# First projection of a two-block network from a feature-major copy of x, with the weight loads at the start of the queue

## The chip, the cores and the metric

One core of one Trainium2 chip runs the kernel. The metric is the device time of one execution in microseconds (us); shorter is better. TensorE is called PE, VectorE DVE, ScalarE ACT, GpSimd POOL, and SyncE, which issues nearly all DMAs here, SP.

## The reference, cut to what matters

256 tokens of 1024 features go through two blocks: an even layer (two attentions of 16 heads), an odd layer (retention) and a second block (state space, window attention, feed-forward). Only the head of the even layer matters here:

```python
def rms_norm(x, g):                       # per token
    y = xf * lax.rsqrt(jnp.mean(xf * xf, axis=-1, keepdims=True) + EPS)
    return y * g
z = rms_norm(x, g_norm) @ w_in            # [256, 1024] @ [1024, 8208]
qa, ka, va, ga, fa, qb, kb, vb, gb = jnp.split(z, cuts, axis=-1)
log_f = jax.nn.log_sigmoid(fa + b_f)      # forget gates, one a head
c = jnp.cumsum(log_f, axis=1)             # added to the logits of attention a, with the causal mask
y = concat([ya * silu(ga), yb * silu(gb)]); x = x + y @ w_out
```

The factor rsqrt(mean(x^2)) belongs to a token, so it can be put in after the product with the weights; the gain g belongs to a feature.

## The kernel before, in words

Every product with weights is done in three: the operands are split into a high part (float32r) and the rest, and high x high, low x high and high x low are summed in PSUM. A weight tile is [128, 1024] float32 (512 KB). `Weights` (lines 48 to 109) streams 233 such tiles in order of use: `load` (L63) issues the DMA on SP into one of five `wraw` buffers, `_prepare` makes the high part `wh` on ACT (L73, `nc.scalar.copy`) and the low part `wl` by a subtraction on DVE (L78; of some tiles on POOL) into a ring of six, and `next` hands a tile out and prepares two ahead. SP's queue holds eight DMAs in flight: a ninth waits for the landing of the first.

The even layer begins with x token-major: `load_x` (L131) brings each tile of 128 tokens in two halves, `norm_transposed` takes the squares (L202 on ACT, L199 on DVE), the factor on POOL (L191), multiplies by factor and gain (L215, the gain spread over the partitions by a product with ones, L598), transposes on PE (L235) and splits into `xTh`, `xTl` [128 features, 8, 256 tokens] (L242, L243). `first_xs` multiplies them by the four tiles of the first half of v (L289 for the high parts of the weights, L296 for their low parts; 48 products of 512 columns), with the second token tile's transposes in between. `forget_gates` follows: a product of 16 rows (24 products, L250 to L252), then a chain over DVE, ACT, DVE (scan, L637), POOL (L639), a DMA to `c_dram` (L640), DMAs back to all partitions (`fox_masks`, L645), and POOL (L648, L649). What it makes, `m`, is added to the scores by the first DVE operation of each head (L346, L348).

Then come, for each quarter i of a half, q, k and gate (`proj_ws`, 48 products of 256 columns each, two weight tiles), and the attention of four heads: scores of a pair (L338), minimum on DVE, exponentials on ACT, normalisation on DVE (L684 to L686), transposes on PE (L362), product with v (L372). Two PSUM banks (`bat`) hold the scores of a pair, so the next pair's scores wait for the DVE operation that reads the last ones (L348). q is scaled on ACT (L664), k copied on DVE (L667), the gate is a tanh on ACT (L670) and one operation on DVE (L671). The framework simulates the program and sets each engine's order of instructions from that; PE executes strictly in its order.

Of the kernel before, what the change touches and what calls it, by code (L numbers as in the profile page):

```python
# [19 lines left out]
P = 128  # L20
# [14 lines left out]
# of this many weight tiles of a part of the network, one has its lower part made on GpSimd (0: none)  # L35
SH = (0, 0, 2, 8)
KE = ("pp", "py")
XH = 2
# [7 lines left out]
class Weights:  # L46
    """Streams weight tiles [128, n] in order of use and splits each into two float32r parts."""

    def __init__(self, tc, raw, par, ahead):
        self.tc, self.nc, self.raw, self.par, self.ahead = tc, tc.nc, raw, par, ahead  # L50
        self.after, self.loaded, self.loads, self.lows = [], [], 0, []
        self.jobs, self.shares, self.done, self.used = [], [], [], 0

    def plan(self, aps, share=0):
        """share: one tile in so many has its lower part computed on GpSimd."""
        self.jobs += aps
        self.shares += [share] * len(aps)

    def load(self):
        ap = self.jobs[self.loads]  # L60
        self.loads += 1
        r = self.raw.tile([P, 1024], F32, tag="raw", name="wraw")
        self.nc.sync.dma_start(r[:, :ap.shape[1]], ap)  # L63
        self.loaded.append(r)

    def _prepare(self):
# [6 lines left out]
        i = nc.scalar.copy(h[:, :n], r[:, :n])  # L73
# [6 lines left out]

    def hold(self, first, second):
# [18 lines left out]
def model_kernel(ctx: ExitStack, tc: tile.TileContext, a: dict, out: bass.AP):  # L100
# [23 lines left out]
    g_row = nrm.tile([P, D], F32, tag="gain", name="g_row")  # L124
    nc.sync.dma_start(g_row[:1, :], a["even_norm"])
    x = [res.tile([P, D], F32, name=f"x{t}") for t in range(2)]

    def load_x(t):
        for h in range(XH):
            sl = slice(h * D // XH, (h + 1) * D // XH)  # L130
            nc.sync.dma_start(x[t][:, sl], a["x"][t * P:(t + 1) * P, sl])  # L131

    load_x(0)
# [36 lines left out]

    w.load()
    load_x(1)

# [20 lines left out]
    def mean_square(src, n, name, eng=None):  # L194
        """Sum of squares over the free dimension of src, divided by n."""
# [9 lines left out]
    def norm_transposed(t, g, th, tl, name, kinds=("pt", "pt"), eng=None, after=None):  # L205
        """The rows of x[t] normalised, times g, its halves, transposed into th, tl."""
        with tc.high_priority():
            xt = x[t]
            parts = [mean_square(xt[:, h * 512:(h + 1) * 512], D, name, eng if h else None) for h in range(2)]
            r = rstd_from(parts, EPS, name)  # L210
            xn = []
            for h in range(2):
                sl = slice(h * 512, (h + 1) * 512)
                xn.append(nrm.tile([P, 512], F32, tag="xn", bufs=3, name="xn"))
                V.scalar_tensor_tensor(xn[h], xt[:, sl], r, g[h], op0=ALU.mult, op1=ALU.mult)  # L215
            return transposed(xn, 8, th, tl, 0, t, kinds, after)

    def gained_transposed(t, g, kinds):
        """The rows of x[t] times g, its halves, transposed into xTh, xTl."""
# [9 lines left out]
    def transposed(src, n, th, tl, k0, t, kinds=("pt", "pt"), after=None):  # L229
        """src, a list of [128 tokens, 512], into th, tl [:, k0.., tokens of tile t] as two float32r parts."""  # L230
        m = min(4, n)
        for b, sb, kind in zip(range(0, n, 4), src, kinds):
            pt = bank(kind)
            for j in range(m):
                i = T.transpose(pt[:, j * P:(j + 1) * P], sb[:, j * P:(j + 1) * P], ident)  # L235
                if after is not None:
                    tc.add_manual_dep(i.ins, after.ins.name, NOSYNC, reason="order")
                    after = None
# [9 lines left out]

    def mm3(ps, lh, ll, rh, rl, first, last):
        T.matmul(ps, lh, rh, start=first, stop=False)  # L250
        T.matmul(ps, lh, rl, start=False, stop=False)  # L251
        T.matmul(ps, ll, rh, start=False, stop=last)  # L252

    def proj_ws(kind="pp"):
        """The next stationary weights times xT: PSUM [128 features, 2, 256 tokens]."""
# [24 lines left out]
    def first_xs(mid):  # L280
        """The first projection: the products of the weights' lower parts last, x's second token tile by mid."""
        tiles = [w.next() for _ in range(4)]
        ps = [bank("pp"), bank("pp")]
        for t in range(2):
            st = slice(t * P, (t + 1) * P)
            for g in range(0, 8, 2):
                for xp in (xTh, xTl):
                    for k in range(g, g + 2):
                        m = T.matmul(ps[t], xp[:, k, st], tiles[k // 2][0][:, 512 * (k % 2):512 * (k % 2) + 512],  # L289
                                     start=xp is xTh and k == 0, stop=False)  # L290
                        if t == 0 and xp is xTh and k == 1:
                            mid(m)
        for t in range(2):
            st = slice(t * P, (t + 1) * P)
            for k in range(8):
                T.matmul(ps[t], xTh[:, k, st], tiles[k // 2][1][:, 512 * (k % 2):512 * (k % 2) + 512],  # L296
                         start=False, stop=k == 7)
# [79 lines left out]
    # Chunks of four steps; two groups (a pair) share the 128 partitions, four pairs are a quarter.  # L377
# [6 lines left out]
    def reduce_angle(r, k, ang):  # L384
        """r: ang minus the nearest multiple of 2 pi; k: scratch."""
# [850 lines left out]
```

## Time and profile before

| | |
|---|---|
| time of three runs | 812.02, 811.92, 810.00 us; median 811.92 |
| span of the profiled execution (first to last instruction) | 810.7 us; its own time is not listed apart, and the median lies 1.2 us above the span |
| PE, share of the span | 96% |
| DVE, ACT, POOL | 69%, 50%, 29% |
| DMA | 146.46 MB, mean 181 GB/s |
| chain of work that ended last | PE 82%, DVE 5%, POOL 4%, issue 3%, ACT 3%, DMA 3% |

The span is cut into 40 slices of 20.3 us; PE's line reads 7, 9, 8 and from then on nearly always 9 or more. A matmul's listed duration includes a modelled end that overlaps with the next one, so how long a series takes is read from the starts. Times in the rows are counted from the span's start.

### The profile page before, as it was taken

How to read it: one execution, taken by the hardware profiler on the slowest of the kernel's cores; microseconds unless marked ns; L12 is line 12 of the kernel's file. 1: busy time of each engine (PE TensorE's matmuls, PEld its weight loads, DVE VectorE, ACT ScalarE, POOL GpSimd, SP SyncE). 2: the span in 40 equal slices, each digit the busy share in tenths (PEclk: the TensorE clock that was granted, in tenths of full speed). 3: DMA queues.
4: the chain of work that ended last, by engine and by line, in shares of the span. 5: the costliest groups of instructions: out<-in, count | busy, mean ns of one | idle time of the engine just before them, and what ended most of it. 6: DMA issues, size and time to landing. Idle time of an engine off the chain costs nothing.

```text
span 810.7 us, 13533 instructions
## 1 busy us (share of the span) xinstructions
PE 780.7 (96%) x5114; PEld 682.1 (84%) x5114; DVE 560.7 (69%) x1013; ACT 408.3 (50%) x680; POOL 237.2 (29%) x274
## 2 busy tenths in 40 slices
PE   7989999999999999999999999989798999999996
PEld 5978997998997789898989887876577999999886
DVE  6987668678778468585766757698849856565433
ACT  5766565457455355344444355736645544443331
POOL 4662111013604212120202006853653322221110
PEclk9999999999999999999999999999999999999999
DMA  7687544644744757453636494852243765555431
GB/s 284 222 270 234 172 165 131 208 150 154 238 161 133 234 186 254 154 188 124 208 119 194 151 334 152 301 195 85 81 127 110 235 200 177 189 183 181 156 130 53
DMA packets 47427, 146.46 MB, mean 181 GB/s; under 512 B 5361, under 2 KB 11777, under 8 KB 47362
## 3 DMA queue, kind: packets, MB, share of 16 engines
q1 hardware_dynamic: 47362, 145.60, 54.5%
q8 instruction: 40, 0.66, 0.3%
q14 instruction: 25, 0.20, 0.1%
HBM read 137.70 MB, written 7.88 MB: 180 GB/s over the span
## 4 chain that ended last, share of the span: by engine, by line
PE 82%; DVE 5%; POOL 4%; issue 3%; ACT 3%; DMA 3%; SPq 0%; POOLq 0%; DVEq 0%; ACTq 0%
PE bpp L274 12%; PE bpp L275 12%; PE bpp L278 12%; PE bpp L251 9%; PE bpp L250 9%; PE bpp L252 9%; PE bat L252 3%; PE bat L251 3%; PE bat L250 3%; PE bpy L372 2%; PE bat L338 2%; PE bpt L362 1%; PE bpp L289 1%; DVE wl L78 1%; POOL wl L78 1%
## 5 line engine op out<-in xcount | busy, mean ns | idle before, releaser
L78 DVE TENSOR_TENSOR wl<-wraw,wh 128x1024 fp32r<-128x1024 f32 x211 | 276.5, 1321 | 114.9 <-ACT wh L73 114.9
L73 ACT CAST wh<-wraw 128x1024 fp32r<-128x1024 f32 (+1 forms) x233 | 238.6, 1045 | 190.0 <-PE bpp L251 54.1
L251 PE MATMUL bpp<-xTl,wh 128*128 128x256 f32 (+1 forms) x680 | 193.3, 284 | 0.0
L250 PE MATMUL bpp<-xTh,wh 128*128 128x256 f32 (+1 forms) x680 | 193.1, 284 | 0.0
L252 PE MATMUL bpp<-xTh,wl 128*128 128x256 f32 (+1 forms) x680 | 192.9, 284 | 0.0
L251 PEld LDWEIGHTS bpp<-xTl,wh 128*128 128x128 f32 (+1 forms) x680 | 127.3, 187 | 2.6 <-issue 1.9
L250 PEld LDWEIGHTS bpp<-xTh,wh 128*128 128x128 f32 (+1 forms) x680 | 127.3, 187 | 1.8 <-issue 1.3
L252 PEld LDWEIGHTS bpp<-xTh,wl 128*128 128x128 f32 (+1 forms) x680 | 127.3, 187 | 1.0 <-issue 0.8
L274 PE MATMUL bpp<-wh,xTh 128*128 128x512 f32 (+1 forms) x288 | 110.9, 391 | 0.8 <-ACT xTh L242 0.8
L275 PE MATMUL bpp<-wl,xTh 128*128 128x512 f32 (+1 forms) x288 | 109.6, 385 | 0.0
L78 POOL TENSOR_TENSOR wl<-wraw,wh 128x1024 fp32r<-128x1024 f32 x22 | 57.7, 2624 | 62.9 <-ACT wh L73 62.9
L278 PE MATMUL bpp<-wh,xTl 128*128 128x512 f32 (+1 forms) x288 | 74.2, 382 | 0.0
L274 PEld LDWEIGHTS bpp<-wh,xTh 128*128 128x128 f32 x288 | 54.5, 190 | 13.3 <-ACT xTh L242 1.7
L275 PEld LDWEIGHTS bpp<-wl,xTh 128*128 128x128 f32 x288 | 54.5, 189 | 11.1 <-DVE wl L78 0.6
L278 PEld LDWEIGHTS bpp<-wh,xTl 128*128 128x128 f32 x288 | 52.2, 188 | 11.1
L274 PE MATMUL bpp<-wh,yh 128*128 128x512 f32 x128 | 50.5, 400 | 0.0
L275 PE MATMUL bpp<-wl,yh 128*128 128x512 f32 x128 | 50.4, 396 | 0.0
L252 PE MATMUL bat<-xTh,wl 128*128 128x256 f32 x160 | 45.1, 282 | 0.0
L250 PE MATMUL bat<-xTh,wh 128*128 128x256 f32 x160 | 45.1, 282 | 0.0
L251 PE MATMUL bat<-xTl,wh 128*128 128x256 f32 x160 | 45.0, 281 | 0.0
L1119 POOL TENSOR_TENSOR gr<-gr,Rh 128x512 f32<-128x512 f32 x10 | 14.3, 1427 | 75.5 <-ACT th L1118 75.5
L278 PE MATMUL bpp<-wh,yl 128*128 128x512 f32 x128 | 35.6, 395 | 0.0
(380 smaller groups left out, 1312.3 us busy)
## 6 DMA issues: line engine op xcount, KB each, us to landing
wraw<-in_w_o SPq DMA_DIRECT2D x40, 512.0 KB, 4.3
wraw<-in_w_gate SPq DMA_DIRECT2D x22, 512.0 KB, 3.8
wraw<-in_w_up SPq DMA_DIRECT2D x22, 512.0 KB, 4.2
wraw<-in_w_dn SPq DMA_DIRECT2D x22, 512.0 KB, 3.7
wraw<-in_w_v SPq DMA_DIRECT2D x16, 512.0 KB, 4.6
wraw<-in_w_g SPq DMA_DIRECT2D x16, 512.0 KB, 4.4
wraw<-in_w_q SPq DMA_DIRECT2D x12, 512.0 KB, 4.1
wraw<-in_w_va SPq DMA_DIRECT2D x8, 512.0 KB, 6.6
```

The source lines that it names most:

```text
L73: i = nc.scalar.copy(h[:, :n], r[:, :n])
L78: self.lows.append(eng.tensor_tensor(lo[:, :n], r[:, :n], h[:, :n].bitcast(F32), op=ALU.subtract))
L250: T.matmul(ps, lh, rh, start=first, stop=False)
L251: T.matmul(ps, lh, rl, start=False, stop=False)
L252: T.matmul(ps, ll, rh, start=False, stop=last)
L274: T.matmul(ps, lh[:, k0 + k, st], wh, start=first and k == 0, stop=False)
L275: T.matmul(ps, lh[:, k0 + k, st], wl, start=False, stop=False)
L278: T.matmul(ps, ll[:, k0 + k, st], wh, start=False, stop=last and k == n - 1)
L289: m = T.matmul(ps[t], xp[:, k, st], tiles[k // 2][0][:, 512 * (k % 2):512 * (k % 2) + 512], start=xp is xTh and k == 0, stop=False)
L338: i = T.matmul(ps[j][:, o], q[rows, qs], k[rows, ks], start=True, stop=True)
L372: i = T.matmul(o[64 * j:64 * j + 64], v[:, b, vc], src, start=b == 0, stop=b == 1)
L1119: G.tensor_tensor(two(gr), two(gr), rep2(Rh), op=ALU.mult)
```

## The change

x comes a second time, from the host as `xT` [128 features, 8, 256 tokens], in five DMAs between the first weight tiles. The gain is a column of eight numbers a partition and is put in as xTh and xTl are made, 16 operations of 128x256 (ACT and DVE). There are no transposes and no norm ahead of the first product. The norm's factor comes in after the products: as `rh` on the partitions for v, as a row `R` [128, 256] for q, k, the gate and the forget gates. The first eight weight tiles go into memory that `yh`, `yl` use later, so they wait for no `wraw` buffer. The first tile and its high part are cut in two. x itself, the masks and the tables of the state space are loaded later. At the start PE multiplies ones with ones, three matmuls (L144 of the changed kernel).

```diff
 class Weights.load:
+        if self.loads in self.given:
+            r = self.given.pop(self.loads)
+        parts = 2 if self.loads == 0 else 1
+        for i in range(parts):
+            m = self.nc.sync.dma_start(r[:, sl], ap[:, sl])
+            if i == 0 and parts > 1:
+                self.between()
...
+    warm = bank("py")
+    for n in (4, 4, 2):
+        T.matmul(warm[:, :n * P]..., ones, ones[:, None, :].to_broadcast([P, n, P]), start=True, stop=True)
...
+    nc.sync.dma_start(g_col, a["even_norm"])
+    def load_xT(k, n=2):
+        nc.sync.dma_start(xT[k // 4][:, k % 4:k % 4 + n, :], a["xT"][:, k:k + n, :])
+    load_xT(0, 1)
-            w.plan(xs("w_v" + m, hf), SH[0] if m + str(hf) != "a0" else 2)
+            w.plan(xs("w_v" + m, hf), SH[0])
...
+    w.given = {j: early[j // 4][:, 1024 * (j % 4):1024 * (j % 4) + 1024] for j in range(8)}
+    w.between = lambda: load_xT(1, 1)
+    for k in (2, 4, 6):
+        w.load()
+        load_xT(k)
+    for _ in range(5):
+        w.load()
...
-    norm_transposed(0, g_even, xTh, xTl, "e0", eng=V)
+    for k in range(8):
+        xk = xT[k // 4][:, k % 4, :]
+        A.activation(xTh[:, k, :], xk, AF.Copy, scale=g_col[:, k:k + 1])
+        V.scalar_tensor_tensor(xTl[:, k, :], xk, g_col[:, k:k + 1], xTh[:, k, :].bitcast(F32),
+                               op0=ALU.mult, op1=ALU.subtract)
...
 first_xs:
+        for g in range(0, 8, 2):
+            tiles.append(w.next())
+            part(g, xTh, 0, first=g == 0)
+            part(g, xTl, 0)
+            if g:
+                part(g - 2, xTh, 1)
+        part(6, xTh, 1, last=True)
...
+                    ps = first_xs()
+                    pf = forget_product()
+                    rs = norm_factors(square_sums())
+                    p0 = proj_ws()
+                    factor_row(rs, last_mm[-1])
-                    A.mul(v[:, t, :], ps[t], 0.5)
+                    A.mul(v[:, t, :], ps[t], rh[t])
-                    A.mul(q.rearrange("p a b -> p (a b)"), ps, -0.125)
+                    V.scalar_tensor_tensor(q, rows(ps), -0.125, rep2(R), op0=ALU.mult, op1=ALU.mult)
-                    V.tensor_copy(k.rearrange("p a b -> p (a b)"), ps)
+                    V.tensor_tensor(k, rows(ps), rep2(R), op=ALU.mult)
-                    A.activation(gs, ps, AF.Tanh, scale=0.5)
-                    V.scalar_tensor_tensor(gs, gs, 1.0, ps, op0=ALU.add, op1=ALU.mult)
+                    V.tensor_tensor(rows(gr), rows(ps), rep2(R), op=ALU.mult)
+                    A.activation(gs, gr, AF.Tanh, scale=0.5)
+                    V.scalar_tensor_tensor(gs, gs, 1.0, gr, op0=ALU.add, op1=ALU.mult)
```

The squares are taken on ACT from xT after the cast of the fifth tile (`square_sums`), summed over the partitions by a product with ones, and the row R is a product of the spread factor with the identity after the first q projection, copied by ACT (`factor_row`).

How the order on the engines moves, at three places. First PE, the start of the program. Before (`bat` is the gain spread, `bpt`, `bpp` and `bpy` with `ident` are transposes of x):

```order
L598 MATMUL bat<-g_row,ones 128x512 x2
L235 MATMUL bpt<-ident,xn 128x128 x8
L289 MATMUL bpp<-wh,xTh 128x512 x2
L289 MATMUL bpp<-wh,xTl 128x512 x2
L235 MATMUL bpp<-ident,xn 128x128 x4
...
L235 MATMUL bpy<-ident,xn 128x128 x4
```

And now:

```order
L144 MATMUL bpy<-ones 128x512 x2
L144 MATMUL bpy<-ones 128x256
L313 MATMUL bpp<-wh,xTh 128x512 x4
L313 MATMUL bpp<-wh,xTl 128x512 x4
...
L313 MATMUL bpp<-wl,xTh 128x512 x4
```

The 16 transposes and the gain's product are gone, and the low parts of the weights come two products of k behind the high ones instead of at the end. Further on in PE's order, 66 products of q, k and gate stood between the scores of the first and of the second pair of heads and 19 between those and the first transposes; now these are 102, and 42 with 3 of the next v.

Second SP, the start of its queue (`early` and `wraw` are weight tiles, `xT_` the copy of x). Before:

```order
L125 DMA g_row<-in_even_norm 1x1024
L131 DMA x_98<-in_x 128x512 x2
L63 DMA wraw<-in_w_va 128x1024
L131 DMA x_99<-in_x 128x512 x2
L63 DMA wraw<-in_w_va 128x1024 x3
L63 DMA wraw<-in_w_fa 128x128
```

And now:

```order
L151 DMA g_col<-in_even_norm 128x8
L159 DMA xT_106<-in_xT 128x256
L69 DMA early<-in_w_va 128x512
L159 DMA xT_106<-in_xT 128x256
L69 DMA early<-in_w_va 128x512
L159 DMA xT_106<-in_xT 128x512
L69 DMA early<-in_w_va 128x1024
L159 DMA xT_107<-in_xT 128x512
...
L69 DMA early<-in_w_fa 128x128
```

Up to the tile of the forget gates (w_fa) the same 3140 KB are asked for, in another order and in smaller pieces. Behind it now come six tiles, bf, the masks, x (two DMAs of 512 KB) and only then the next tiles.

Third ACT, around the factor row `Re` (R), now:

```order
L729 ACTIVATE v<-bpp,rh_298 128x512
L729 ACTIVATE v<-bpp,rh_304 128x512
L86 CAST wh<-wraw 128x1024
L713 COPY Re<-bpt 128x256
L86 CAST wh<-wraw 128x1024
L459 ACTIVATE sm_dt<-ssm_par 128x16
L86 CAST wh<-wraw 128x1024
L658 ACTIVATE az_f<-az_f 16x256
```

There was no R before; it stands behind the cast of the twelfth tile, the first of the next quarter's q, and the chain of the forget gates (`az_f`) stands behind it.

## Rows read from the trace of the kernel before

**Rows 1.** Parts 1 and 2 of the profile's page: busy time, share and instructions of each engine; then PE's busy tenths in the 40 slices.

```profile
PE 780.7 (96%) x5114; PEld 682.1 (84%) x5114; DVE 560.7 (69%) x1013; ACT 408.3 (50%) x680; POOL 237.2 (29%) x274
PE   7989999999999999999999999989798999999996
```

**Rows 2.** Stretches of the start: bounds, length, busy time of PE, PEld, DVE, ACT, POOL (and instructions), PE's granted clock, DMA share, GB/s.

```profile
0.00:5.00 5.00, 2.60 (x3) 1.16 (x4) 1.12 (x8) 2.01 (x3) 2.38 (x12) 1.00 0.47 169
5.00:10.00 5.00, 3.11 (x10) 1.57 (x8) 2.76 (x6) 1.73 (x4) 0.55 (x1) 1.00 0.92 329
10.00:15.00 5.00, 3.93 (x11) 3.18 (x12) 4.68 (x7) 4.37 (x8) 2.93 (x2) 1.00 0.95 330
```

**Rows 3.** PE in order of time, 2 to 45 us: start, length, line, operation, count, and in brackets the idle time before and what ended it.

```profile
2.40 3.75 PE L598 MATMUL bat<-g_row,ones 1*128 1x512 f32 x4 [2.40 <-DMA g_row<-in_even_norm]
7.36 1.97 PE L235 MATMUL bpt<-ident,xn 128*128 128x128 f32 x8 [1.22 <-DVE xn L215]
11.07 1.22 PE L289 MATMUL bpp<-wh,xTh 128*128 128x512 f32 x2 [1.74 <-ACT xTh L242]
...
12.94 1.05 PE L235 MATMUL bpp<-ident,xn 128*128 128x128 f32 x4
...
15.24 0.60 PE L235 MATMUL bpy<-ident,xn 128*128 128x128 f32 x4
15.60 0.71 PE L289 MATMUL bpp<-wh,xTh 128*128 128x512 f32 x2
...
19.40 0.63 PE L289 MATMUL bpp<-wh,xTl 128*128 128x512 f32 x2
19.86 0.64 PE L289 MATMUL bpp<-wh,xTh 128*128 128x512 f32 x2
...
26.93 0.28 PE L252 MATMUL bpp<-xTh,wl 128*16 128x256 f32 x1
...
27.73 0.28 PE L250 MATMUL bpp<-xTh,wh 128*128 128x256 f32 x1
27.84 0.28 PE L251 MATMUL bpp<-xTl,wh 128*128 128x256 f32 x1
...
44.93 0.28 PE L251 MATMUL bpp<-xTl,wh 128*128 128x256 f32 x1
```

**Rows 4.** DMAs of the start: two issues on SP in order of time (start, length), then, each from the stretch in which it was issued, what was loaded, count, KB and us from issue to landing: the second token tile's second half, the first weight tile, the tile of the forget gates.

```profile
2.00 0.43 SPq L63 DMA_DIRECT2D wraw<-in_w_va  x1
2.47 0.91 SPq L131 DMA_DIRECT2D x<-in_x  x2
5.40 0.76 SPq L63 DMA_DIRECT2D wraw<-in_w_fa  x1
...
x<-in_x SPq DMA_DIRECT2D x2, 256.0 KB, 6.5
wraw<-in_w_va SPq DMA_DIRECT2D x1, 512.0 KB, 6.2
wraw<-in_w_fa SPq DMA_DIRECT2D x1, 64.0 KB, 8.2
```

**Rows 5.** PE between 45 and 62 us, in order of time, as in rows 3: the scores of the first and second pair, the products after them, the first transposes.

```profile
45.38 0.93 PE L338 MATMUL bat<-k,q 64*128 64x128 f32 x8
46.23 0.39 PE L251 MATMUL bpp<-xTl,wh 128*128 128x256 f32 x1
...
56.16 0.93 PE L338 MATMUL bat<-k,q 64*128 64x128 f32 x8 [1.82 <-DVE nm L348]
57.24 0.27 PE L252 MATMUL bpp<-xTh,wl 128*128 128x256 f32 x1
57.35 0.28 PE L250 MATMUL bpp<-xTh,wh 128*128 128x256 f32 x1
...
61.14 0.33 PE L362 MATMUL bpt<-ident,s 128*128 128x128 f32 x1 [1.61 <-DVE s L685]
```

**Rows 6.** The chain of the forget gates in order of time on DVE, ACT, POOL and SP, as in rows 3.

```profile
36.84 1.28 ACT L634 ACT_TABLE_LOAD   x1
38.13 0.51 ACT L634 ACTIVATE az_f<-az_f,ones 16x256 f32<-16x256 f32 x1
42.87 0.67 DVE L637 TENSOR_TENSOR_SCAN c_f<-ones,z_f 16x256 f32<-16x256 f32 x1
43.60 2.27 POOL L639 COPY c_f<-c_f 16x256 f32<-16x256 f32 x1 [1.20 <-DVE c_f L637]
54.64 0.29 DVE L346 CUSTOM_DVE_ANT_0 s<-bat,m 128x128 f32<-128x128 f32 x1 [3.73 <-POOL m L648]
56.02 0.08 DVE L348 DVE_READ_ACCUMULATOR2_ANT nm<- 128x1 f32 x1
```

**Rows 7.** Durations: the cast of a tile and its low part at the page's list (count, busy us, mean ns); then a product of a PSUM tile with a row spread over it on DVE, from the feed-forward (count, shortest/median/longest ns).

```profile
L78 DVE TENSOR_TENSOR wl<-wraw,wh 128x1024 fp32r<-128x1024 f32 x211 | 276.5, 1321 | 114.9 <-ACT wh L73 114.9
L73 ACT CAST wh<-wraw 128x1024 fp32r<-128x1024 f32 (+1 forms) x233 | 238.6, 1045 | 190.0 <-PE bpp L251 54.1
L1117 DVE TENSOR_TENSOR gr<-bpp,R x10: 683/684/689, 635.8 to 737.9; 128x512 f32<-128x512 f32 x10
```

**Rows 8.** Stretches of the even layer, columns as in rows 2.

```profile
27.70:195.00 167.30, 163.86 (x1257) 146.60 (x1256) 129.06 (x321) 98.65 (x196) 50.53 (x62) 1.00 0.60 193
180.00:200.00 20.00, 20.00 (x126) 16.32 (x124) 16.94 (x51) 11.81 (x28) 9.63 (x23) 1.00 0.48 158
```

More of the change, by code (lines that the diff above doesn't have):

```diff
@@ L36 @@
 SH = (0, 0, 2, 8)
-KE = ("pp", "py")
-XH = 2
 KO = (("pt", "pt"), ("at", "at"))
@@ L52, in __init__ @@
         self.jobs, self.shares, self.done, self.used = [], [], [], 0
+        self.issued, self.given, self.casts = [], {}, []
     def plan(self, aps, share=0):
@@ L72, in _prepare @@
         lo = self.par.tile([P, 1024], F32R, tag="wl", name="wl")
-        i = nc.scalar.copy(h[:, :n], r[:, :n])
+        if not self.done:
+            nc.scalar.copy(h[:, :n // 2], r[:, :n // 2])
+            i = nc.scalar.copy(h[:, n // 2:n], r[:, n // 2:n])
+        else:
+            i = nc.scalar.copy(h[:, :n], r[:, :n])
+        self.casts.append(i)
         if self.after:
@@ L122, in model_kernel @@
     V.memset(ones, 1.0)
-    g_row = nrm.tile([P, D], F32, tag="gain", name="g_row")
-    nc.sync.dma_start(g_row[:1, :], a["even_norm"])
+    warm = bank("py")
+    for n in (4, 4, 2):
+        T.matmul(warm[:, :n * P].rearrange("p (a b) -> p a b", a=n), ones, ones[:, None, :].to_broadcast([P, n, P]),
+                 start=True, stop=True)
+    warm = const.tile([P, 1], F32, name="warm")
+    A.copy(warm, ones[:, :1])
     x = [res.tile([P, D], F32, name=f"x{t}") for t in range(2)]
+    g_col = const.tile([P, 8], F32, name="g_col")
+    nc.sync.dma_start(g_col, a["even_norm"])
+    xT = [nrm.tile([P, 4, S], F32, tag="gain", name=f"xT{h}") for h in range(2)]
     def load_x(t):
[L129 to L133, printed above, removed]
+        w.issue_after(10, nc.sync.dma_start(x[t], a["x"][t * P:(t + 1) * P, :]))
+    def load_xT(k, n=2):
+        nc.sync.dma_start(xT[k // 4][:, k % 4:k % 4 + n, :], a["xT"][:, k:k + n, :])
+    load_xT(0, 1)
     w = Weights(tc, wraw, wpar, 2)
@@ L203, in mean_square @@
         return s
[L205 to L216, printed above, removed]
     def gained_transposed(t, g, kinds):
@@ L234, in transposed @@
             for j in range(m):
[L235 to L238, printed above, removed]
+                T.transpose(pt[:, j * P:(j + 1) * P], sb[:, j * P:(j + 1) * P], ident)
             pv = pt[:, :m * P].rearrange("p (j t) -> p j t", j=m)
@@ L251, in mm3 @@
         T.matmul(ps, lh, rl, start=False, stop=False)
-        T.matmul(ps, ll, rh, start=False, stop=last)
+        last_mm[:] = [T.matmul(ps, ll, rh, start=False, stop=last)]
     def proj_ws(kind="pp"):
@@ L278, in mm_xs, with first_xs, part @@
                 T.matmul(ps, ll[:, k0 + k, st], wh, start=False, stop=last and k == n - 1)
-    def first_xs(mid):
-        tiles = [w.next() for _ in range(4)]
+    def first_xs():
         ps = [bank("pp"), bank("pp")]
[L284 to L297, printed above, removed]
+        tiles = []
+        def part(g, xp, j, first=False, last=False):
+            for k in range(g, g + 2):
+                for t in range(2):
+                    T.matmul(ps[t], xp[:, k, t * P:(t + 1) * P],
+                             tiles[k // 2][j][:, 512 * (k % 2):512 * (k % 2) + 512],
+                             start=first and k == g, stop=last and k == g + 1)
+        for g in range(0, 8, 2):
[5 more added lines that the diff above has]
+        part(6, xTh, 1, last=True)
         return ps
@@ L593, in tables_quarter @@
         nc.sync.dma_start(y_dram[i][:, QT0:], t0.rearrange("p s c -> p (s c)"))
-    g_even = [bank("at") for h in range(2)]
-    for h in range(2):
-        T.matmul(g_even[h], ones[:1, :], g_row[:1, h * 512:(h + 1) * 512], start=True, stop=True)
-    norm_transposed(0, g_even, xTh, xTl, "e0", eng=V)
-    def second_tile(after):
-        norm_transposed(1, g_even, xTh, xTl, "e1", KE, None, after)
-    lctx = ExitStack()
-    ypool = lctx.enter_context(tc.tile_pool(name="ypool", bufs=1))
+    for k in range(8):
[3 more added lines that the diff above has]
+                               op0=ALU.mult, op1=ALU.subtract)
     def y_tiles():
@@ L650, in fox_masks, with square_sums @@
             return m0, m1
+        rh = []
+        R = evc.tile([P, S], F32, name="Re")
+        def square_sums():
+            sq = [ev.tile([P, 512], F32, tag=n, name="sq_e") for n in ("q", "k", "q", "k")]
+            for j in range(4):
+                i = A.activation(sq[j], xT[j // 2][:, 2 * (j % 2):2 * (j % 2) + 2, :].rearrange("p a b -> p (a b)"),
+                                 AF.Square, scale=1.0 / math.sqrt(D))
+                tc.add_manual_dep(i.ins, w.casts[4].ins.name, NOSYNC, reason="order")
+            V.tensor_tensor(sq[0], sq[0], sq[1], op=ALU.add)
+            V.tensor_tensor(sq[2], sq[2], sq[3], op=ALU.add)
+            V.tensor_tensor(sq[0], sq[0], sq[2], op=ALU.add)
+            V.tensor_tensor(sq[1][:, :S], sq[0][:, :S], sq[0][:, S:], op=ALU.add)
+            return sq[1][:, :S]
@@ new lines, in norm_factors, with factor_row @@
+        def norm_factors(sm):
+            pr = bank("pt")
+            rs = []
+            for t in range(2):
+                T.matmul(pr[:, t:t + 1], sm[:, t * P:(t + 1) * P], ones[:, :1], start=True, stop=True)
+            for t in range(2):
+                rs.append(rstd_from([pr[:, t:t + 1]], EPS, "e"))
+                rh.append(evc.tile([P, 1], F32, name=f"rh{t}"))
+                V.tensor_scalar(rh[t], rs[t], 0.5, None, op0=ALU.mult)
+            return rs
+        def factor_row(rs, after):
+            pr = bank("pt")
+            for t in range(2):
+                rb = ev3.tile([P, P], F32, tag="s", bufs=5, name="rb_e")
+                V.tensor_copy(rb, rs[t].to_broadcast([P, P]))
+                i = T.matmul(pr[:, t * P:(t + 1) * P], rb, ident, start=True, stop=True)
+                tc.add_manual_dep(i.ins, after.ins.name, NOSYNC, reason="order")
+            A.copy(R, pr[:, :S])
```

51 lines of the change are left out of this document (35 added, 16 removed).

## The prediction, as it was made before the result was known

> **What bounds the kernel now.** I read the page first: PE is busy for 780.7 of 810.7 us, and its line of slices is full from the fourth on but for a stretch near the middle and the end [rows 1]. So only time in which PE does nothing useful can be won, and the first three slices hold some of it. Then the stretches of the start: PE is busy 2.60 and 3.11 us in the first two stretches of 5 us [rows 2]. PE's order of time says with what: the gain's spread at 2.40, transposes at 7.36, and the first product with weights only at 11.07, after a wait for xTh [rows 3]. The first q projection starts at 27.73. All that follows is the same work before and after the change, so what counts is how much earlier it starts and what PE waits for behind it. Two such waits are there: 1.82 us before the second pair's scores at 56.16 and 1.61 us before the first transposes at 61.14 [rows 5], both behind the DVE operation that waited 3.73 us for the masks `m` of the forget gates [rows 6]. From 62 us to the end of the even layer PE has no listed wait: in 27.7 to 195 us it is busy for 163.86 of 167.30, and 3.4 of the missing are those two [rows 8].
>
> **Term 1, the earlier start.** The first product needs 388 KB of DMA (the gain column, one k of xT, half a weight tile) and two operations of ACT; before it needed x, the norm and the transposes. But the rest of the data comes no faster than the queue gives it. In the trace the first weight tile, issued at 2.00 with 1028 KB up to and with it, landed 6.2 us later, at 8.2; the second token tile's second half (1540 KB, issued at about 2.9) at 9.4; the forget gates' tile (3140 KB) at 5.40 + 8.2 = 13.6 [rows 4]. In the new order 1540 KB is the second weight tile and 3140 KB again the forget gates' tile. So I set the second weight tile at 9.4 and the fourth just ahead of 13.6.
>
> The Trainium skill (DMA: Bandwidth & Descriptors, Latency and other measured facts) gives an HBM latency of 0.2 us on average but 2 us at high load, which speaks against asking for nine tiles at once; the late landings agree, since bytes alone at the rate of the rows would put 1540 KB at 7.2.
>
> From bytes alone it is 0.85 MB by 5 us and 329 GB/s after [rows 2], so (1.58 - 0.85) / 0.329 = 2.2 us past 5, 7.2. I take 9.4, the landing of the same number of bytes, and keep 7.2 as the other end. Cast of 1.05 [rows 7]: 10.45. By then the eight products of the first tile are done (0.85 MB have moved by 5 us [rows 2], twice what the first product needs). The 40 left are 40 x 0.23 = 9.3 us, by the spacing of 19.40 to 19.86 [rows 3]: 19.8. The later tiles don't hold them up: the fourth is cast by 14.7, and its products are due after 24 x 0.23 = 5.6 us, at 16.0. The forget gates' 24 products, at (27.73 - 26.93) / 7 = 0.114 [rows 3], end at 22.5; four small products for the norm add some 0.3 in all. **The q projection starts at 22.5 to 22.7 in place of 27.73: 5.0 us.**
>
> What hides the rest: the 16 operations that make xTh and xTl, some 0.4 us each on either engine, lie under the DMA, as do the squares (ACT is free from the cast of the forget gates' tile at about 15, and their sum is needed behind the third q product at about 22.9). The sums' product is placed there in PE's order; if the squares were 3 us later, PE would wait for them. The two low parts that POOL made come to DVE, whose queue at this point holds little else.
>
> Bounds of term 1. Above: second tile at 7.2, so 2.2 us more, 7.2 in all. Below: TensorE's clock. The granted clock reads 1.00 in all stretches of the start [rows 2], the upper level of 2.4 GHz, but the products tell another story: from 11.07 to 15.60 PE did eight products and eight transposes in 4.53 us, where 8 x 0.23 + 8 x 0.11 = 2.7 is the pace reached at 15.24 [rows 3]. So 1.8 us went to the low level before, after a pause from 9.33 to 11.07. The ones times ones give PE work from about 1.1 us on: by the four records of 0.94 each of the gain's spread [rows 3], two per matmul of 512 columns, five take 4.7 us, to 5.8 or, if the clock rises under them, earlier.
>
> The Trainium skill (TensorE: Matmul & The Clock Gate, What's actually happening) says that the array's default is the throttled state and that activity lifts it; that agrees with the spacings and not with the granted-clock column, and it speaks both for the ones and against the pauses for tiles that follow them.
>
> After the first tile's eight products PE pauses up to 2 us. In the trace a pause of 1.82 us before 56.16 was followed by products at 0.11 [rows 5], so I take the full pace; if the clock falls, the 1.8 us are paid again and term 1 is 3.1. Because PE may still be busy with ones at 5.8, the first product can be late by 0.8; nothing comes of it, as the second tile is not there.
>
> **Term 2, the wait for the masks.** Their chain now begins with R. R is copied by ACT behind the cast of the twelfth tile, and that tile is 8.2 MB down the queue: 2.5 MB by 10 us, then 330 GB/s [rows 2], 27.3, plus the 1.4 us by which the forget gates' tile was late against bytes alone (13.6 against 12.2): 28.7; cast and copy, R at 30.1. Nothing waits for R on PE itself: v frees two PSUM banks without it, and the third is due at 22.7 + 17.1 = 39.8. Then the chain, by the order of DVE and ACT: the cast of the fourteenth tile (9.8 MB, 33.7) ends at 34.7, exponential and others 0.6, the table 1.28 and the logarithm 0.51 [rows 6], a cast 1.05 and a low part 1.2 ahead of the scan, which starts at about 39.8 (before: 42.87). From the scan to the first DVE operation with masks it was 54.64 - 42.87 = 11.8 and 1.5 more to the last [rows 6]: 51.6 and 53.1.
>
> On PE the three projections take 144 x 0.1187 = 17.1 ((44.93 - 27.84) / 144) [rows 3], so the first scores are at 40.0; then 0.9 for them [rows 5] and 102 products of 0.1187: the second scores are due at 53.0. The masks come at the same moment. The first transposes stand 45 products later, at about 59; they were ready 5.1 us after the last masked operation [rows 5, 6], 58.2. So nearly all of the 3.43 us goes; I take **3.0**. What is late next is the same chain: each us by which R or a cast is late costs PE one.
>
> Bounds of term 2: 3.43 above. Below: masks at 54.6 as before make PE wait from 53.0 to 56.1, which leaves 0.3; three us later still, term 2 is -2.7.
>
> **Term 3, DVE.** q moves from ACT to DVE and the gate gets a product with R: 16 operations of 0.684 [rows 7], 10.9 us until the layer's end, less than DVE's pauses (167.3 - 129.1 = 38 in 27.7 to 195) [rows 8]. Most of these are waits for casts that wait for PE. Even from 180 to 200 DVE has 3 us free of 20 [rows 8], and gets some 1.4 more. Zero, with PE's order set anew; I leave 0 to 1 for it in the range. Behind the even layer PE's order is the same but for a few rows, so nothing is given back.
>
> **Sum.** 810.7 - 5.0 - 3.0 = 802.7 for the span; the median of the runs is 1.2 above the span shown, so **803.9 us**.
>
> **Rivals.**
> *The start is held.* The tiles land later than their byte counts say, or the clock falls in the pauses: term 1 is 1.5 to 3.1. For it: eight DMAs in flight from the first us, and 2.2 us late already in the trace. Against: no more bytes stand ahead than before. Price: 811.9 - 2.3 - 3.0 = 806.6.
> *The masks come no earlier.* R waits for loads that I put at 28.7, and the chain runs in step with them. For it: the new dependence on R. Against: POOL's copy behind the scan was slow (2.27) with other work around it, and is first in line now. 811.9 - 5.0 - 0.3 = 806.6 too; together with the first, 809.3.
> *DVE becomes the bound* (the other side). If in each quarter DVE's two new operations end last ahead of the scores, all 10.9 us come to PE's path: 811.9 - 8.0 + 10.9 = 814.8. It decides from the point where DVE's pauses in a quarter (about 20 us of it) are under 1.4 us; they are 3 us in the fullest stretch shown, so it is unlikely.
> *The change doesn't do what it says.* The second and third tiles land at 13 to 14, since all nine share the engines; then PE starts early, stops, and reaches the q projection at 26 to 27: 811.
>
> **How the numbers follow.** The forecast has a chance of 0.60, the held start 0.13, the late masks 0.13 (both of them within these), DVE 0.06, no early data 0.08. The forecast's own bounds: 7.2 + 3.4 = 10.6 gives 801.3, and somewhat more if the second tile is even earlier; 4 + 2 gives 805.9. The range takes in the single rivals and both together: 800.0 to 809.5, which leaves out the last two and little more. A measurement of this kernel can tell about 0.3%, 2.4 us, from no change: faster is below 809.5. Faster 0.84 (the first three cases less a little), same 0.10 (no early data, and both rivals at their worst), slower 0.06.
>
> **What would show it.** First product at 5 to 6 us; eight products before the second tile's cast, whose end is at 10 to 10.5; spacing 0.23 from there; first product of 128 x 128 x 256 at 22 to 23; R copied at about 30; the scan before 41; no PE wait over 1 us between 50 and 62; no new one to 250; DVE about 13 us busier in all. I am wrong if the q projection starts after 25, if PE waits for `nm` or `s` again as long as before, or if waits on q or the gate appear on PE.

## The result and the profile after

The changed kernel is slower. Four runs gave 815.52 to 817.25 us, median 815.99; four of the kernel before in the same session gave 811.19: ratio 1.006, 95% interval 1.0041 to 1.0078. In a later session of twelve runs it was 816.81 against 813.02, ratio 1.004 (1.0021 to 1.006). The forecast was 803.9. The profiled execution took 815.52, its span 813.7.

From the page of the changed kernel, part 1, then PE's busy tenths and its granted clock in the 40 slices:

```profile
PE 786.4 (97%) x5108; PEld 686.5 (84%) x5108; DVE 570.5 (70%) x1038; ACT 411.7 (51%) x679; POOL 214.3 (26%) x272
...
PE   8998899999999999999999999989798999999996
...
PEclk9999899999999999999999999999898999999998
```

Against [rows 1] the first slices are fuller, as intended, but the fourth and the fifth are not: an 8 stands where there was a 9, and the clock line has an 8 in the fifth. PE in order of time (start, length, line, operation, count, idle time before and what ended it):

```profile
1.03 3.86 PE L144 MATMUL bpy<-ones 128*128 128x512 f32 x6 [1.03 <-DVE pw_i L498]
5.27 0.73 PE L313 MATMUL bpp<-wh,xTh 128*128 128x512 f32 x2 [0.38 <-ACT wh L83]
7.61 1.22 PE L313 MATMUL bpp<-wh,xTh 128*128 128x512 f32 x2 [1.60 <-ACT wh L84]
...
11.07 1.20 PE L313 MATMUL bpp<-wh,xTh 128*128 128x512 f32 x4 [0.53 <-ACT wh L86]
12.11 1.09 PE L313 MATMUL bpp<-wh,xTl 128*128 128x512 f32 x4
13.04 1.09 PE L313 MATMUL bpp<-wl,xTh 128*128 128x512 f32 x4
...
23.25 0.28 PE L274 MATMUL bpp<-xTh,wh 128*128 128x256 f32 x1
...
41.35 0.93 PE L364 MATMUL bat<-k,q 64*128 64x128 f32 x8
...
54.50 0.93 PE L364 MATMUL bat<-k,q 64*128 64x128 f32 x8
...
61.41 0.33 PE L388 MATMUL bpt<-ident,s 128*128 128x128 f32 x1
...
78.97 0.28 PE L275 MATMUL bpp<-xTl,wh 128*128 128x256 f32 x1
83.52 0.90 PE L388 MATMUL bpt<-ident,s 128*128 128x128 f32 x3 [4.27 <-ACT pT L390]
...
84.43 0.41 PE L274 MATMUL bpp<-xTh,wh 128*128 128x256 f32 x1
84.64 0.41 PE L275 MATMUL bpp<-xTl,wh 128*128 128x256 f32 x1
...
88.91 0.41 PE L274 MATMUL bpp<-xTh,wh 128*128 128x256 f32 x1
...
90.69 0.28 PE L274 MATMUL bpp<-xTh,wh 128*128 128x256 f32 x1
90.81 0.28 PE L275 MATMUL bpp<-xTl,wh 128*128 128x256 f32 x1
...
105.19 0.93 PE L364 MATMUL bat<-k,q 64*128 64x128 f32 x8
```

Read it in three steps. Behind the ones (from 1.03) the first product runs at 5.27, the second tile's at 11.07, and from there they stand 0.23 apart ((13.04 - 12.11) / 4). The q projection starts at 23.25 instead of 27.73 [rows 3], and the scores of the first two pairs and the first transposes follow without the waits of [rows 5]. At 79 PE stops for 4.27 us, a wait that the kernel before does not have. And behind it the products of 256 columns stand 0.213 us apart (84.43 to 84.64), to 89, where they stand 0.12 apart at 90.69: the clock fell. The stretches say the same (columns as in rows 2; the granted clock is the third number from the right):

```profile
27.70:195.00 167.30, 162.92 (x1218) 145.21 (x1217) 136.15 (x363) 99.59 (x193) 35.92 (x66) 0.98 0.58 189
60.00:80.00 20.00, 19.14 (x110) 14.43 (x108) 17.95 (x61) 12.23 (x27) 6.13 (x10) 1.00 0.52 171
80.00:100.00 20.00, 16.48 (x118) 15.03 (x119) 15.63 (x35) 15.79 (x28) 1.68 (x3) 0.83 0.75 250
83.50:89.20 5.70, 5.68 (x26) 5.51 (x26) 3.78 (x13) 5.67 (x12) 0.20 (x1) 0.50 0.95 308
```

In 83.5 to 89.2 PE reads as busy for 5.68 of 5.70 us, at a granted clock of 0.50, the level of 1.2 GHz: busy time alone would not have shown the loss. The Trainium skill (TensorE: Matmul & The Clock Gate, What's actually happening) calls the low level the array's default, which activity lifts; this stretch agrees.

What PE waits for is a copy by ACT (`pT`, L390). So the next view is ACT in order of time:

```profile
73.89 1.28 ACT L487 ACT_TABLE_LOAD   x1
75.18 1.06 ACT L487 ACTIVATE trig<-trig 128x1024 f32<-128x1024 f32 x1
76.26 1.28 ACT L381 ACT_TABLE_LOAD   x1
77.55 0.40 ACT L381 ACTIVATE s<-s,nm 128x128 f32<-128x128 f32 x1
...
78.45 1.98 ACT L86 CAST wh<-wraw 128x1024 fp32r<-128x1024 f32 x2
80.44 1.28 ACT L487 ACT_TABLE_LOAD   x1
81.73 1.06 ACT L487 ACTIVATE trig<-trig 128x1024 f32<-128x1024 f32 x1
82.70 0.39 ACT L352 CAST yh<-o 128x256 fp32r<-128x256 f32 x1
82.99 0.47 ACT L390 COPY pT<-bpt 128x384 f32<-128x384 f32 x1
...
86.33 1.28 ACT L381 ACT_TABLE_LOAD   x1
```

The same work in the kernel before:

```profile
48.41 1.28 ACT L461 ACT_TABLE_LOAD   x1
49.70 2.01 ACT L461 ACTIVATE trig<-trig 128x1024 f32<-128x1024 f32 x2
51.62 1.03 ACT L73 CAST wh<-wraw 128x1024 fp32r<-128x1024 f32 x1
52.67 1.28 ACT L355 ACT_TABLE_LOAD   x1
```

`trig` are two buffers of angles for the rotation of the states in the second block, whose sines ACT takes in passing. Sine and exponential need different tables, and a change of table is an instruction of 1.28 us. Before, both sines stood together at 49.7, under one load, ahead of the exponentials. In the new order they stand among the exponentials of the third and fourth pair of heads, and apart: four loads from 73.89 to 87.6, 5.1 us, where two stood before. The copy at 82.99 stands behind two casts, a load, a sine and a cast, from 78.45 on, and PE has nothing in its order that could go first.

The account of the two profiled executions, whose spans are 3.0 us apart while the medians are 4.8 apart, from starts of PE's rows (fifth scores: those of the fifth pair of heads; `kd`: transposes in the second block, first at 538.50 and 539.41; last row: 803.90 and 806.76):

| stretch | before | after | difference |
|---|---|---|---|
| to the q projection | 27.73 | 23.25 | -4.48 |
| to the first scores | 17.65 | 18.10 | +0.45 |
| to the fifth scores | 59.17 | 63.84 | **+4.67** |
| to `kd` in the second block | 433.95 | 434.22 | +0.27 |
| to the last row | 265.40 | 267.35 | +1.95 |
| sum | 803.90 | 806.76 | +2.86 |

One edit of the change bears on the new place of the sines: the parameters of the state space (`ssm_par`), from which the angles are made, are now loaded behind the thirteenth weight tile, issued at 20.88 instead of 9.58. Before, DVE finished the angles of the second buffer at 47.2, ahead of both sines; now it makes them in between its work for the heads and finishes at 75.5, when the first sine has begun (first row before, second row after):

```profile
46.83 0.41 DVE L397 TENSOR_SCALAR trig<-trig 128x512 f32<-128x512 f32 x1
...
75.08 0.42 DVE L423 TENSOR_SCALAR trig<-trig 128x512 f32<-128x512 f32 x1
```

No run puts that load back alone, so it is not shown that this sets the sines apart.

### The profile page after: what moved, and what is told of

It is laid out like the page before. It is cut to its first block, busy times and chain, and to the rows that moved or that the text cites. A ratio compares the mean times of both kernels' runs of the same rounds, so it can differ in the third digit from the quotient of the medians.

```text
span 813.7 us, 13549 instructions
## 1 busy us (share of the span) xinstructions
PE 786.4 (97%) x5108; PEld 686.5 (84%) x5108; DVE 570.5 (70%) x1038; ACT 411.7 (51%) x679; POOL 214.3 (26%) x272
## 5 line engine op out<-in xcount | busy, mean ns | idle before, releaser
L92 DVE TENSOR_TENSOR wl<-wraw,wh 128x1024 fp32r<-128x1024 f32 x205 | 268.8, 1321 | 104.4 <-ACT wh L86 104.0
L86 ACT CAST wh<-wraw 128x1024 fp32r<-128x1024 f32 x225 | 231.4, 1048 | 186.6 <-PE bpp L275 59.9
L276 PE MATMUL bpp<-xTh,wl 128*128 128x256 f32 x672 | 192.5, 286 | 0.0
L274 PE MATMUL bpp<-xTh,wh 128*128 128x256 f32 x672 | 192.1, 286 | 0.0
L275 PE MATMUL bpp<-xTl,wh 128*128 128x256 f32 x672 | 191.7, 285 | 0.0
L274 PEld LDWEIGHTS bpp<-xTh,wh 128*128 128x128 f32 x672 | 127.8, 190 | 2.2 <-issue 1.8
L276 PEld LDWEIGHTS bpp<-xTh,wl 128*128 128x128 f32 x672 | 127.7, 190 | 1.5 <-issue 1.5
L275 PEld LDWEIGHTS bpp<-xTl,wh 128*128 128x128 f32 x672 | 127.7, 190 | 1.0 <-issue 0.7
L92 POOL TENSOR_TENSOR wl<-wraw,wh 128x1024 fp32r<-128x1024 f32 x20 | 51.1, 2555 | 62.2 <-ACT wh L86 62.2
```

The costliest lines, as they stand in the source:

```text
L92: self.lows.append(eng.tensor_tensor(lo[:, :n], r[:, :n], h[:, :n].bitcast(F32), op=ALU.subtract))
L276: last_mm[:] = [T.matmul(ps, ll, rh, start=False, stop=last)]
```

## The experiments

Three theories at first. A: the large sines among the exponentials, by their table loads and the clock that falls in the wait. B: DVE, with its new operations, sets the pace of the quarters. C: the loss lies in the second block, where the last stretch is 1.95 longer. Four sessions; each compares with runs of the kernel before in the same session (811.19, 811.68, 813.02, 812.58 us), so ratios are compared, not times. Starts of PE's rows in the profiled executions, in us:

```
                                q      1st     5th   5th-1st    kd    kd to  median  ratio to before
                               proj.  scores  scores                  last          (95% interval)
before                         27.73  45.38  104.55   59.17  538.50  265.40  811.19
after                          23.25  41.35  105.19   63.84  539.41  267.35  815.99  1.0060 (1.0041-1.0078)
e1  copies, not large sines    23.72  41.82  100.00   58.18  534.26  268.37  809.85  0.9972 (0.9957-0.9986)
e2  sines under one load       25.79  43.89  102.34   58.45  536.57  267.22  810.54  0.9976 (0.9958-0.9994)
e3  no ones                    25.53  43.63  107.27   63.64  541.46  267.35  815.22  1.0033 (1.0013-1.0053)
e4  before, sines apart        28.32  45.96  107.66   61.70  541.61  267.23  815.02  1.0037 (1.0018-1.0055)
e5  after again                27.38  45.49  109.30   63.81  543.55  267.25  816.81  1.0040 (1.0021-1.0060)
e6  before, copies             27.20  44.84  103.22   58.38  537.16  266.07  813.86  1.0013 (0.9998-1.0027)
e7  copies, no ones            26.53  44.64  101.80   57.16  536.02  267.19  810.49  0.9969 (0.9953-0.9985)
e8  complete, angles first     22.79  40.86   99.31   58.45  533.54  265.21  808.33  0.9942 (0.9922-0.9962)
e9  e8 again                   23.15  41.22   99.55   58.33  533.78  265.36  809.78  0.9952 (0.9933-0.9971)
e10 e8 without ones            23.29  41.36   99.71   58.35  533.94  267.17  811.07  0.9974 (0.9958-0.9991)
e11 e1 again                   25.44  43.55  100.77   57.22  534.99  265.43  807.93  0.9934 (0.9912-0.9956)
e12 e11 with more ones         25.20  42.90  100.85   57.95  535.04  265.14  809.45  0.9958 (0.9940-0.9976)
```

**e1.** The large sines replaced by copies, which need no table (the states' rotation is left out of the result by that):

```diff
-        for t in trig + [sm]:
-            A.activation(t, t, AF.Sin)
+        for t in trig:
+            A.activation(t, t, AF.Copy)
+        A.activation(sm, sm, AF.Sin)
```

> The changed kernel, but the two large sines (trig, 128x1024) are copies, so their four table loads (1.28 us each) are not there; the states' rotation is left out with that. Theory A (the table loads among the exponentials hold up the softmax, PE waits 4.3 us at 79 to 83.5 and then runs 5.7 us at the low clock): no PE wait over 1 us between 70 and 100 us, granted clock 1.00 there, 6 to 7 us less than the changed kernel: 809 to 810. Rival B (DVE has too much to do in the even layer, the tables only happen to be there): within 1.5 us of the changed kernel, 814.5 to 817, PE waits for DVE in the same stretch. Rival C (the second block's clock is what costs): gap to the kernel before stays at 2 us or more whatever happens at 80 us.

809.85 us, and the fifth scores 58.18 behind the first. From 80 to 100 us PE is busy again, at full clock:

```profile
80.00:100.00 20.00, 19.67 (x164) 17.90 (x162) 16.52 (x36) 12.95 (x27) 5.78 (x6) 1.00 0.83 300
```

A holds for the stretch that lost the time. DVE keeps all its operations there, so B falls. The last stretch, 268.37, is even longer than after, and the kernel still is faster than before, so C falls as the main cause.

**e2.** The sines kept, all under one load (the added dependences set an order on ACT and no more):

```diff
+        i1 = A.activation(trig[1], trig[1], AF.Sin)
+        i0 = A.activation(trig[0], trig[0], AF.Sin)
+        tc.add_manual_dep(i0.ins, i1.ins.name, NOSYNC, reason="order")
+        i2 = A.activation(sm, sm, AF.Sin)
+        tc.add_manual_dep(i2.ins, i0.ins.name, NOSYNC, reason="order")
```

> The changed kernel with the three sines ordered one behind the other, so that ACT loads the sine table once (as late as the first of the large ones was) instead of three times. Theory A: two of the four loads in the softmax stretch go and so does the load ahead of the first softmax; PE's wait at 79 shrinks from 4.3 to 1 to 2.5 us, 3 to 6 us less than the changed kernel: 810 to 813. Rival B: no change, 815 to 817. Rival C: no more than 2 us less.

810.54: a complete kernel, faster than before by 0.2% although its profiled execution started the q projection only at 25.79. The large sines still stand at 78 to 80 us, but with one load ahead of them and one behind: PE's wait for `pT` there is 0.7 us.

```profile
82.83 0.44 PE L388 MATMUL bpt<-ident,s 128*128 128x128 f32 x2 [0.74 <-ACT pT L390]
```

**e3.** The three products of ones removed (L142 to L145 of the changed kernel).

> The changed kernel without the three matmuls of ones. If they earn the full clock for the first products: the first tiles' products stand 0.43 to 0.51 us apart for some 3 us, q starts 1 to 2 us later (24.3 to 25.3 in place of 23.25) and the time is 816.5 to 818. Rival (the second tile's load covers it): q within 0.5 us of 23.25, time within 1 us of the changed kernel. Neither theory on the sines expects a difference at 80 us.

The q projection came at 25.53, later than the 24.3 to 25.3 expected, and the wait at 80 was there (4.29 us). The time, ratio 1.0033, is not above that of the change (1.006 and 1.004, intervals overlap), as the rival had it.

**e4.** Meant as the converse: the kernel before, with one sine behind the exponentials of the fifth head and one behind the sixth:

```diff
+            ex.append(A.activation(p[:, P:], s[:, P:], AF.Exp, ...))
...
+        for t, h in ((trig[0], 4), (trig[1], 5)):
+            i = A.activation(t, t, AF.Sin)
+            tc.add_manual_dep(i.ins, ex[h].ins.name, NOSYNC, reason="order")
```

> The kernel before with only the places of its two large sines moved, behind the exponentials of the fifth and the sixth head, as the changed kernel has them. Theory A: four table loads come into the softmax stretch, PE waits 3 to 5 us there and may fall to the low clock: 814 to 818 against 811. Rivals B and C: nothing else was added to any engine, so within 1 us of the kernel before.

815.02, 3.3 us above before. But its profile does not show the sines doing it: the wait of 3 to 5 us is missing. The moved loads and sines stand from 75.67 to 84.8, and the third to the fifth scores, which take them in, are 34.42 us apart, before 34.37, without a listed wait of PE. The loss in the profile, 2.57 us, lies ahead of them, between the second and the third scores (16.59 against 14.02). PE, ACT, and 60 to 80 us with columns as above:

```profile
62.21 0.33 PE L362 MATMUL bpt<-ident,s 128*128 128x128 f32 x1 [2.18 <-DVE s L687]
...
75.67 1.28 ACT L461 ACT_TABLE_LOAD   x1
...
60.00:80.00 20.00, 17.52 (x114) 15.09 (x114) 15.15 (x41) 13.56 (x28) 4.07 (x6) 0.91 0.57 187
```

The wait at 62.21 is the second one of [rows 5], 0.57 us longer. Behind it the products of 256 columns stand 0.213 us apart until 67.1; in the kernel before they kept 0.12. Why the wait is longer is not settled. So this run shows that the edit makes the kernel before slower, but not that the sines' new place does it, and it can't stand as the converse of e1 and e2. The last stretch is 265.40 to 267.23 in the three profiles of kernels with the start of before and 265.14 to 268.37 in the eleven with the new start, so its 1.95 us cannot be put down to the change.

**e5.** The changed kernel again, unedited.

> The changed kernel as it stands, in one session with the next three. Both theories: 815 to 817 us, the wait of about 4.3 us at 80 us again, and the granted clock at half for some 5 us behind it. If the wait were not there in this execution and the time the same, the account by the sine tables would fall.

The wait of 4.27 us is there again, ending at 87.48, and the fifth scores are 63.81 behind the first, to 0.03 us as in the first profile. What differs is the start: the q projection at 27.38, as late as before the change. PE and a stretch of that start:

```profile
7.60 0.74 PE L313 MATMUL bpp<-wh,xTh 128*128 128x512 f32 x2 [1.40 <-ACT wh L84]
...
12.29 2.08 PE L313 MATMUL bpp<-wh,xTh 128*128 128x512 f32 x4 [2.28 <-ACT wh L86]
14.16 1.91 PE L313 MATMUL bpp<-wh,xTl 128*128 128x512 f32 x4
15.87 1.91 PE L313 MATMUL bpp<-wl,xTh 128*128 128x512 f32 x4
```

```profile
10.00:17.50 7.50, 5.22 (x13) 4.13 (x13) 6.10 (x10) 6.83 (x13) 0.00 (x0) 0.50 1.03 410
```

The second tile was cast 1.2 us later than in the first profile (PE at 12.29 against 11.07), PE waited 2.28 us for it instead of 0.53, and its products then took 0.47 and 0.43 instead of 0.23 until about 18 us. So the rival of the held start is real, in some executions and not in others.

**e6.** The kernel before with e1's copies (same part left out).

> Kernel before with a copy in the place of the two large sines (it leaves out the sines of the states' rotation). Theory A (the swaps cost the changed kernel most because of where they stand): before had them on ScalarE at 48 to 54 us, where 1.8 us of waits on scores and transposes followed, so it gains 0 to 2: 809.5 to 811.5, and the start of the change is worth that less the time of the changed kernel with the same edit (809.85): 0 to 2 us. Rival D (the start's 4 to 5 us arrive at the end in full, and the missing part is the sines' own): about 814, slower than before, which nothing but a clock could do. Rival E (the kernel is held elsewhere, in the second block): within 0.3 us of before.

Ratio 1.0013 (0.9998 to 1.0027): no gain, the least that A allowed, and what E expected; D's 814, which is 1.0029 of the session that it was worked out from, lies just outside. Where they stood, the sines cost the kernel before nothing that the runs can tell. With e1 and e11 this prices the rest of the change without any large sine on either side: 0.9972 / 1.0013 and 0.9934 / 1.0013, 3.3 and 6.4 us, an estimate across sessions.

**e7.** e1 without the ones.

> The changed kernel with that copy and without the three products of ones. In the execution without ones the first projection stood 2.3 us later. Theory A, in which the start's gain arrives where the stall at 80 us is gone: 809.85 plus about 2, 811 to 812.5. Rival F (what the ones buy at the start is taken back later, the table stall or not): 809.5 to 810.2.

0.9969 against e1's 0.9972: F, not A. The q projection is 2.8 us later than in e1 (26.53 against 23.72), the fifth scores only 1.8, as the stretch between holds fewer small waits (57.16 against 58.18). The rest of the difference is within what the executions differ by.

**e8.** The complete kernel with the angles and sines given to the scheduler at high priority:

```diff
+        with tc.high_priority():
             trig = [nrm.tile([P, 2, 512], F32, tag="gain", name="trig") for _ in range(2)]
             ...
             for t in trig + [sm]:
                 A.activation(t, t, AF.Sin)
```

> The changed kernel, complete, with the tables' angles and sines given to the scheduler at high priority: the small sine ahead of the first exponential, and both large sines next to each other under one load in the midst of the second heads' exponentials. Theory A: two loads fewer in the stretch at 73 to 88 us, 809.5 to 812.5; the more it lies above 810.5 the more the one remaining swap holds the exponentials. Rival B (VectorE's order in that stretch holds it): 815 or more.

808.33, ratio 0.9942: faster than before, faster than theory A had it, and in the same session 8.5 us below the change (816.81). ACT's table loads and sines in it:

```profile
47.24 1.28 ACT L488 ACT_TABLE_LOAD   x1
48.53 0.26 ACT L488 ACTIVATE sm_trig<-sm_trig 128x64 f32<-128x64 f32 x1
49.75 1.28 ACT L381 ACT_TABLE_LOAD   x1
...
70.02 1.28 ACT L488 ACT_TABLE_LOAD   x1
71.31 2.01 ACT L488 ACTIVATE trig<-trig 128x1024 f32<-128x1024 f32 x2
...
74.27 1.28 ACT L381 ACT_TABLE_LOAD   x1
```

The large sines stand together, and PE's listed waits from 60 to 100 us are 0.9 and 0.5. The Trainium skill (ScalarE: Activation LUTs, Table sets: the hidden batching unit) tells to batch activations by table set; after, e2 and e8 agree, with 1.28 us a load and far more than that by what stands behind it.

**e9 and e10.** e8 again, and e8 without the ones.

> The kernel with the sines ahead of the heads (e8) once more, in one session with the next three. It stood 4.7 us under the kernel before. Theory A: 4 to 5.5 us under before again. If it is within 2 us of before, the earlier session was luck of the clock.

> The same without the three products of ones; no other order changes. Theory G (the ones buy what the traces show at the q projection, 2 to 3 us, once nothing behind it waits): 2 to 3 us slower than e9. Rival F (it is given back later): within 1 us of e9.

e9 repeats e8 in the ratio, 0.9952, 3.9 us; its median is 2.8 us under before, less than the 4 to 5.5 expected. e10 lies 1.3 us above it, between G and F, and the intervals overlap (0.9933 to 0.9971 and 0.9958 to 0.9991): what the ones are worth stays open. Without them the ratio is lower by 0.0007 to 0.0027 in e3, lower by 0.0003 in e7 and higher by 0.0022 in e10. e10's profiled execution had the q projection at 23.29, nearly as early as with ones, so its profile does not show their worth either.

**e11 and e12.** e1 again, and with two more products of ones behind the first tile's:

```diff
+            i = part(g, xTl, 0)
+            if not g:
+                fill = bank("py")
+                for _ in range(2):
+                    f = T.matmul(fill..., ones, ones[:, None, :].to_broadcast([P, 4, P]), start=True, stop=True)
+                    tc.add_manual_dep(f.ins, i.ins.name, NOSYNC, reason="order")
```

> The kernel with copies in place of the large sines (e1) once more, as the base of the next one: 1.5 to 3 us under the kernel before.

> That kernel with two more products of ones (512 columns each) behind the first tile's eight products, where PE waits 0.5 to 3.0 us for the second tile. Theory H (the spread of the start, q at 22.8 to 27.4, is the granted clock that falls in this wait): no stretch of the first 20 us under 0.95, q at 23 to 24.5, and 0 to 2 us less than e11. If the wait alone decided, not the clock behind it, q would be as late as without them, and the time the same or up to 1 us more.

e11 came at 0.9934, its median 4.6 us under before where 1.5 to 3 were expected. e12 missed what H expected: the granted clock was 0.89 in the first 10 us, the q projection came at 25.20, the time is not below e11's. PE had waited 2.24 us for the second half of the first tile already and came out of that at the low level, at which the two products of ones ran from 10.93 to 12.39, 0.7 us past the end of the second tile's cast at 11.65. The edit also moved rows further on. H is neither shown nor refuted by it.

## Why the prediction was wrong, point by point

- **The step that failed** is the end of term 3: "Zero, with PE's order set anew", no new PE wait to 250 us, "nothing is given back". The order had been compared on PE, on SP and on ACT around R; the order of ACT behind that, where the table loads had moved, was not priced. It holds four loads and two sines in 14 us ahead of copies that PE needs. In the profile the stretch is 4.67 us longer than before. Against the same order without the large sines it is more: from the third to the fifth scores the profiles with the sines apart (after, e3, e5) have 38.8 to 38.9 us, those with copies in their place (e1, e7, e11) 32.1 to 32.4. Of these 6.4 to 6.9 us the wait is 4.27, and the 23 products behind it at 0.213 in place of 0.12 are about 2. Undoing the step (e1, e2, e8) takes some 5 to 8.5 us off the time of the change. e4 does not show the converse.
- Term 1 forecast q at 22.5 to 22.7; the first profile has 23.25, with the second tile's products at 11.07 against 10.45. But seven profiles of kernels with this start read 22.79, 23.15, 23.25, 23.72, 25.44, 25.79 and 27.38. Their wait for the second tile was 0.89, 1.14, 0.53, 1.74, 2.53, 3.04 and 2.28 us; with the first four the products behind it ran at 0.23, with the last three they began at 0.46. The forecast named this ("if the clock falls") and put 3.1 as the bound; it differs from execution to execution. The mean of the seven is 24.5, which makes term 1 3.2 in place of 5.0; in one it was 0.35, and in three q started after 25, the forecast's own sign of being wrong.
- Term 2's chain came as worked out, by ACT and DVE of the changed kernel in order of time:

```profile
30.07 0.38 ACT L713 COPY Re<-bpt 128x256 f32<-128x256 f32 x1 [0.90 <-PE bpt L711]
...
39.93 0.91 DVE L662 TENSOR_TENSOR_SCAN c_f<-ones,z_f 16x256 f32<-16x256 f32 x1
...
50.26 0.29 DVE L372 CUSTOM_DVE_ANT_0 s<-bat,m 128x128 f32<-128x128 f32 x1 [0.63 <-POOL m L673]
```

  R is copied at 30.07 (forecast 30.1), the scan starts at 39.93 (39.8), the first masked operation at 50.26 (51.6). The two waits of [rows 5] are gone. Yet only part of the 3.0 arrived: without the sines' stall the first to fifth scores take 57.2 to 58.5 us against 59.17 (58.38 in e6), with four more products of 0.12 in them, and new waits of up to 1 us show (0.9 and 0.5 in e8); some 0.7 us of e8's stretch stays open. The forecast asked what is late next only of the masks.
- Term 3's own subject was right: DVE's busy time grew by 9.8 us (about 13 forecast), no wait on q or the gate appeared on PE, and the long stretch from the fifth scores to `kd` grew by 0.27.
- The rival of DVE as the bound has nearly the measured time (814.8), by a mechanism that isn't there.

So the sum of e8 is what the forecast's terms were worth: -4.94 to the q projection, +0.42, -0.72, +0.28, -0.19, in all -5.15 in place of -8.0. That is one profile, with the earliest start of the seven; the ratios of e8 and e9 give -4.7 and -3.9.

Not settled: why the framework's simulated order sets the sines apart in the changed kernel (shown is only that priority for their angles joins them), what makes e4 slower, and the ones' worth.

## What to carry to other kernels

Where a scheduler sets the order, an edit at the start can move instructions on any engine a hundred rows later; read the new order of every engine whose copies the bound engine needs, and count in it the table loads and long instructions that have come ahead of such a copy. An engine that is half idle can still stop the bound one for 4 us. And a wait of PE costs more than its length where the clock falls behind it: here 4.27 us, and about 2 more in the products that followed.

## What was unexpected of the hardware

After the wait of 4.27 us PE ran at a granted clock of 0.50 for some 5.7 us while doing dense products. At the start the same kernel began its q projection at 23.25 in one execution and at 27.38 in another, by the pace behind the waits for the first two tiles. Their length alone does not decide: the wait of 1.60 us at 7.61 in the first profile was followed by products at about 0.45 (four in 1.91), one of 1.58 at the same place in e8 by products at 0.23. Twelve runs of the change spread over 811.99 to 819.54 us. And in 500 to 640 us, where PE has many waits, the mean granted clock was 0.99 in the profile of before and 0.95 in that of after, without an edit to the program there.
